# Ordering the experts on the chip, two of them with 64 slots and two products

## The chip, the cores and the metric

One NeuronCore of a Trainium2 chip. The metric is the device time of one execution, in microseconds (us). The kernel before takes 1795.38 us, the median of 3 runs (1792.59 to 1796.04). For times this close, a difference below 0.2% counts as no difference.

## The reference

Three transformer blocks run one after the other over 256 tokens of width 1024, in float32. The change touches one layer, the mixture of experts in the second block. A router gives each token its two best of 8 experts; each expert is a gated network with three weight matrices:

```python
D_FF, N_EXPERTS, TOP_K = 2816, 8, 2
logits = xt @ router_w                       # 256 tokens x 8 experts
top_val, top_idx = lax.top_k(logits, TOP_K)
gates = softmax(top_val)
# for each expert e, the tokens xb that chose it:
y = (silu(xb @ w1[e]) * (xb @ w3[e])) @ w2[e]
out[token] += gate * y
```

There are 512 pairs of a token and an expert. With these inputs the reference's router gives experts 0 to 7 the counts 27, 81, 40, 116, 33, 68, 72 and 75. All weights of all experts are read: 3 x 1024 x 2816 x 4 bytes x 8, 276.8 MB.

## The kernel before

**Three products for a float32.** TensorE multiplies in a reduced form of float32 here (shown as fp32r). So each operand is split in two parts, hi (the value rounded to that form) and lo (what is left), and `mm3` makes three products: hi x hi, lo x hi, hi x lo. Every weight tile must be split on the way: a DMA brings a raw tile of 128x1024 (a *unit*, half a megabyte), ACT casts it to hi (L715), DVE subtracts to get lo (L716), and PE then makes the products (L741 to L743).

**One expert.** Its tokens are gathered into 128 slots by products with a 0/1 matrix (`gather`, tiles bx). The 22 blocks of 128 hidden columns are taken in 6 groups (five of 4 blocks, one of 2). A group has a first product with w1 (4 units, into the PSUM tile ab), one with w3 (4 units), the gate (`silu` on ACT, L1730, and `hidden` on DVE, L1735), a turning of the 128 slots' hidden values by 4 transposes (`turn`, L1686, then a split into the tile hp by L811 on ACT and L812 on DVE), and a second product with w2 (`second`, 4 units, into acc). The second product of a group is recorded after the first products of the next one. The step from one `hidden` to the next is called a *turn* here: 12 units. At an expert's end the result is split (yp), scattered back to the tokens by products (L1695), and added with its gate on DVE (L1696).

**What sets the order.** The experts come as 0, 1, ..., 7. `in_order` chains the instructions of PE, ACT and DVE in the order in which the program records them, so each of these engines works its queue in that order; POOL and the DMA queue are not in the chains. `Units.take` records the split of a unit some four units ahead of its products, since there are 4 buffers for hi and 4 for lo. Raw tiles have about 20 buffers; SP issues their DMAs (L464, L471) as they come free, so the raw tiles are far ahead.

**A second pass** (`tc.If(cnt > P)`) takes an expert's tokens beyond 128; with the counts above it isn't entered.

Of the kernel before, what the change touches and what calls it, by code (L numbers as in the profile page):

```python
# [12 lines left out]
I32 = mybir.dt.int32  # L13
# [105 lines left out]
def t5_bucket(n):  # L119
# [11 lines left out]
    "cm": [("trilT", 128), ("iota128", 128), ("iota8", 8)],  # L131
# [11 lines left out]
def constants():  # L143
# [19 lines left out]
    put("iota128", np.broadcast_to(1 + np.arange(P, dtype=f), (P, P)))  # L163
    put("iota8", np.broadcast_to(np.arange(8, dtype=f), (P, 8)))
# [134 lines left out]
class RouterX:  # L299
# [77 lines left out]
    def route(s, fill):  # L377
# [3 lines left out]
        s.m8, ix, ixf = keep([P, 2, 8]), keep([P, 2, 8], U32), keep([P, 2, 8])  # L381
        o12, s.AmR, s.pos = keep([P, 2, 2, 8]), keep([P, 2, 8], F32R), keep([P, 2, 8])
# [19 lines left out]
        fill(3)  # L402
        ps = k.mm([P, 2, 8])
# [18 lines left out]
    def count(s):

        k, nc = s.k, s.k.nc
        s.ci, cf, pc = s.keep([P, 1], I32), s.keep([P, 1]), k.mm([P, 8])
        for t in range(2):
            nc.tensor.matmul(pc, lhsT=s.ones, rhs=s.AmR[:, t], start=(t == 0), stop=(t == 1))
        nc.vector.tensor_reduce(cf, pc, axis=AX.X, op=ALU.max)
        nc.vector.tensor_copy(s.ci, cf)


class Units:
# [3 lines left out]
    def __init__(s, k):  # L436
        T = k.A["moe"]
        s.k, s.early, s.where, s.n, s.loaded, s.ready = k, {}, {}, 0, 0, []
        s.todo = []
        todo2 = []  # L440
        for e in range(NE):
            u = 0
            for g0 in range(0, FF // P, 4):
                n = min(4, FF // P - g0)
                for i in range(2 * n):
                    s.todo.append((T[e, u + i // 2], i % 2, 8 // n, n * P, i % n * (8 // n)))
                u += n
                s.todo += todo2
                todo2 = [(T[e, u + i // 2], i % 2, 1, D, g0 + i) for i in range(n)]
                u += n // 2  # L450
        s.todo += todo2

    def load(s, n, pool=None):
        src, i, kp, w, _ = s.todo[n]
        k, cs = s.k, slice(i * D, i * D + D)
        s.loaded = max(s.loaded, n + 1)
# [5 lines left out]
        if i == 0 and isinstance(at, Halves) and n + 1 not in s.early and n + 1 not in s.where:  # L462
# [4 lines left out]
            s.early[n + 1] = (raw[:, D:], *s.todo[n + 1][2:4])  # L467
# [70 lines left out]
class K:  # L538
# [163 lines left out]
    def split(s, raw, kper, n, pad=0, to=None):  # L702
# [13 lines left out]
        nc.vector.tensor_tensor(out=lo[:, :m], in0=raw[:, :m], in1=hi[:, :m].bitcast(F32), op=ALU.subtract)  # L716
# [747 lines left out]
    def block2b(s):  # L1464
        with ExitStack() as st:
# [7 lines left out]
            with s.phase("gm", b8=2, b2=2, ring=(ring, 10), ps=dict(mm=InTurn(ps[:4]), acc=InTurn(ps[4:6]), fil=InTurn(ps[6:]))):  # L1473
# [4 lines left out]
                nc.gpsimd.memset(keep([P, 72]), 0.0)  # L1478
# [6 lines left out]
            with s.phase("moe", b1=3, ps=dict(mm=InTurn(ps[:2]), ab=InTurn(ps[2:6]), acc=InTurn(ps[6:])), extra=(("bx", 4),)):  # L1485
                s.raws = raws
                s.sh, s.hp, s.yp = [InTurn([b4[i]]) for i in (0, 1, 3)]

                units.where = {units.loaded + len(raws) + i: p for i, p in enumerate((s.yp, InTurn(b4[2:3])))}
# [607 lines left out]
```

## Time and profile before

| | |
|---|---|
| median of 3 runs | 1795.38 us |
| the profiled execution | 1799.04 us, of which the span of the trace is 1797.2 us |
| stage of the experts' products | about 640 to 1417 us in the span |
| PE, DVE, ACT, POOL busy over the span | 1763.1, 1387.8, 1136.7, 94.5 us |
| bytes moved by DMA | 446.51 MB |

The span is the time from the first instruction to the last; the profiled execution has 1.8 us more around it and stands 3.7 us above the median. Engines are PE (TensorE's products), PEld (its weight loads, beside PE), DVE, ACT and POOL; SP issues the DMAs. A long kernel is read by stages: `windows` give each engine's busy time in a stretch, `waits` say who waited for whom, and timelines list single instructions with their start and length. Lengths of neighbours on one engine overlap a little, since an engine starts on the next instruction before the last one's results are all written; so what one costs in a full queue is the distance of starts, not the length.

### The profile page before, as it was taken

The numbers are of one execution on the slowest core, as the hardware profiler recorded it, in microseconds if no ns is written. First come the engines' busy times: TensorE is split into PE (matmuls) and PEld (weight loads), VectorE is DVE, ScalarE is ACT, GpSimd is POOL, SyncE is SP. The second block draws the span as 40 slices with busy tenths as digits, with TensorE's granted clock in tenths as the row PEclk, the third lists the DMA queues.
The fourth block names the chain that finished last, engine by engine and source line by source line (L and its number), as shares of the span: only waits on it lengthen the run. The fifth ranks groups of instructions, "written<-read, shape, count | busy, mean of one in ns | idle before, by whom it ended". The sixth has DMA issues, their size and how long they took to land. (4 is left out here: it accounts for less than half of the span.)

```text
span 1797.2 us, 26971 instructions
## 1 busy us (share of the span) xinstructions
PE 1763.1 (98%) x10129; PEld 1530.3 (85%) x10129; DVE 1387.8 (77%) x2013; ACT 1136.7 (63%) x1566; POOL 94.5 (5%) x102
## 2 busy tenths in 40 slices
PE   8999999999999999999999999999999899999998
PEld 7889879899987888888888888888888688889997
DVE  6576779755567689999989899999999788865544
ACT  6355656644456478777777787777878665554443
POOL 1100010101000110000000000000000020001101
PEclk9899999999999999999999999999999899999999
DMA  8535463856647679999999999998997444257540
GB/s 288 179 129 165 147 197 118 272 177 192 201 133 258 260 264 362 359 368 337 360 358 369 347 345 371 353 383 319 370 369 285 157 147 153 71 175 250 185 141 24
DMA packets 127947, 446.51 MB, mean 248 GB/s; under 512 B 11304, under 2 KB 23856, under 8 KB 96960
## 3 DMA queue, kind: packets, MB, share of 16 engines
q1 hardware_dynamic: 127808, 444.71, 69.0%
q8 instruction: 81, 1.33, 0.3%
q14 instruction: 58, 0.48, 0.1%
HBM read 443.61 MB, written 2.63 MB: 248 GB/s over the span
## 5 line engine op out<-in xcount | busy, mean ns | idle before, releaser
L716 DVE TENSOR_TENSOR lo<-raw,hi 128x1024 fp32r<-128x1024 f32 (+1 forms) x828 | 987.7, 1223 | 299.5 <-ACT hi L715 289.1
L715 ACT CAST hi<-raw 128x1024 fp32r<-128x1024 f32 (+1 forms) x828 | 852.4, 1048 | 436.7 <-PE mm L743 129.7
L741 PE MATMUL ab<-hi,bx 128*128 128x512 f32 (+1 forms) x768 | 290.7, 378 | 0.0
L743 PE MATMUL ab<-lo,bx 128*128 128x512 f32 (+1 forms) x768 | 286.0, 372 | 0.0
L742 PE MATMUL ab<-hi,bx 128*128 128x512 f32 (+1 forms) x768 | 285.6, 372 | 0.0
L741 PE MATMUL mm<-Xh,hi 128*128 128x256 f32 x760 | 213.9, 281 | 2.2 <-DVE Xl L815 2.2
L743 PE MATMUL mm<-Xl,hi 128*128 128x256 f32 x760 | 213.5, 281 | 0.0
L742 PE MATMUL mm<-Xh,lo 128*128 128x256 f32 x760 | 213.4, 281 | 0.0
L743 PEld LDWEIGHTS ab<-lo,bx 128*128 128x128 f32 x768 | 144.6, 188 | 25.8
L742 PEld LDWEIGHTS ab<-hi,bx 128*128 128x128 f32 x768 | 145.0, 189 | 23.7
L741 PEld LDWEIGHTS ab<-hi,bx 128*128 128x128 f32 x768 | 144.9, 189 | 23.7
L743 PEld LDWEIGHTS mm<-Xl,hi 128*128 128x128 f32 x760 | 145.7, 192 | 0.1
L741 PEld LDWEIGHTS mm<-Xh,hi 128*128 128x128 f32 x760 | 142.9, 188 | 3.3 <-ACT hi L715 2.5
L742 PEld LDWEIGHTS mm<-Xh,lo 128*128 128x128 f32 x760 | 143.1, 188 | 0.9
L741 PE MATMUL acc<-hi,hp 128*128 128x512 f32 x352 | 137.3, 390 | 0.0
L742 PE MATMUL acc<-hi,hp 128*128 128x512 f32 x352 | 137.1, 390 | 0.0
L743 PE MATMUL acc<-lo,hp 128*128 128x512 f32 x352 | 136.9, 389 | 0.0
L741 PE MATMUL fil<-Xh,hi 128*128 128x256 f32 (+1 forms) x352 | 101.8, 289 | 1.3 <-ACT b L1986 0.5
L743 PE MATMUL fil<-Xl,hi 128*128 128x256 f32 (+1 forms) x352 | 100.3, 285 | 0.0
L742 PE MATMUL fil<-Xh,lo 128*128 128x256 f32 (+1 forms) x352 | 100.3, 285 | 0.0
L743 PEld LDWEIGHTS acc<-lo,hp 128*128 128x128 f32 x352 | 66.1, 188 | 13.9
L741 PEld LDWEIGHTS acc<-hi,hp 128*128 128x128 f32 x352 | 66.1, 188 | 13.1
(496 smaller groups left out, 2796.2 us busy)
## 6 DMA issues: line engine op xcount, KB each, us to landing
raw<-in_moe_dram SPq DMA_DIRECT2D x240, 1024.0 KB, 7.1
raw<-in_ffn_w_dram SPq DMA_DIRECT2D x66, 512.0 KB, 4.5
raw<-in_moe_dram SPq DMA_DIRECT2D x48, 512.0 KB, 6.6
raw<-in_a_w_in_dram SPq DMA_DIRECT2D x24, 512.0 KB, 4.4
raw<-in_w_gate_dram SPq DMA_DIRECT2D x22, 512.0 KB, 4.4
raw<-in_w_up_dram SPq DMA_DIRECT2D x22, 512.0 KB, 4.8
raw<-in_w_down_dram SPq DMA_DIRECT2D x22, 512.0 KB, 3.7
raw<-in_w_in_odd_dram SPq DMA_DIRECT2D x20, 512.0 KB, 4.7
```

The source lines that it names most:

```text
L715: nc.scalar.copy(hi[:, :m], raw[:, :m])
L716: nc.vector.tensor_tensor(out=lo[:, :m], in0=raw[:, :m], in1=hi[:, :m].bitcast(F32), op=ALU.subtract)
L741: nc.tensor.matmul(out, lhsT=lh, rhs=rh, start=start, stop=False, skip_group_check=skip)
L742: nc.tensor.matmul(out, lhsT=ll, rhs=rh, start=False, stop=False, skip_group_check=skip)
L743: nc.tensor.matmul(out, lhsT=lh, rhs=rl, start=False, stop=stop, skip_group_check=skip)
```

## The change

Four things change in the stage of the experts.

- **Order on the chip.** Experts 0 and 1 keep their places. The other six are ordered by the number of their tokens, fewest first (`order`), and the gates, positions and counts are made again for the new places. SP loads the six numbers into registers, and weight addresses follow from them.
- **Narrow experts.** Those at places 2 and 3 (here experts 4 and 2, with 33 and 40 tokens) get 64 slots. The hi parts of their 64 slots and the lo parts stand side by side in one operand of 128 columns, so `prods` makes two products (with hi and with lo of the weights) where `mm3` makes three. The two halves are added when the hidden values are turned: 8 products with a folding matrix take the place of 4 transposes, and the gate comes after it, on 64 slots.
- **Pairs in turn.** The places are taken in the pairs (0, 1), (2, 4), (5, 6), (3, 7), and the two of a pair take turns group by group, so a narrow group and a wide one alternate in the second and the fourth pair. ab has 2 PSUM banks instead of 4, acc 4 instead of 2.
- **Every eighth subtraction on POOL.** `fetch` gives the subtraction for lo of units 7, 15, 23, ... to POOL instead of DVE: 66 of 528.

The second pass is entered where a wide expert has more than 128 tokens or a narrow one more than 64.

```diff
@@ Units.fetch, split @@
-            hi, lo = s.k.split(*(s.early.pop(s.n, None) or s.load(s.n, s.where.get(s.n))))
+            k = s.k
+            hi, lo = k.split(*(s.early.pop(s.n, None) or s.load(s.n, s.where.get(s.n))),
+                             sub=k.nc.gpsimd if s.n % 8 == 7 else k.nc.vector)
...
-        nc.vector.tensor_tensor(out=lo[:, :m], in0=raw[:, :m], in1=hi[:, :m].bitcast(F32), op=ALU.subtract)
+        (sub or nc.vector).tensor_tensor(out=lo[:, :m], in0=raw[:, :m], in1=hi[:, :m].bitcast(F32), op=ALU.subtract)
@@ the order of pairs and groups @@
+PAIRS = ((0, 1), (2, 4), (5, 6), (3, 7))
+NARROW = (2, 3)
+GROUPS = [(g, min(4, FF // P - g)) for g in range(0, FF // P, 4)]
+TURNS = [(pair, i, g, n) for pair in PAIRS
+         for i, (g, n) in [(i, g) for g in GROUPS[:-2] for i in range(2)] + [(i, g) for i in range(2) for g in GROUPS[-2:]]]
@@ RouterX @@
+    def order(s):
+        k, nc = s.k, s.k.nc
+        s.ci, s.ix = s.keep([P, 1], I32), s.keep([P, 8], U32)
+        key, top, by = k.ts(8), k.ts(8), k.ts(8)
+        nc.vector.tensor_tensor(out=key, in0=k.c("rank"), in1=s.counts(), op=ALU.subtract)
+        nc.vector.max(top, key)
+        nc.vector.max_index(s.ix, top, key)
+        nc.vector.tensor_copy(by, s.ix)
+        nc.vector.tensor_tensor(out=s.o12, in0=by[:, None, None, :].to_broadcast([P, 2, 2, 8]),
+                                in1=s.ixf[:, :, 0:2, None].to_broadcast([P, 2, 2, 8]), op=ALU.is_equal)
+        nc.vector.tensor_tensor(out=s.AmR, in0=s.o1, in1=s.o2, op=ALU.add)
+        s.shares()
...
+    def experts(s):
+        s.of = [0, 1] + [s.k.nc.values_load(s.ix[0:1, c:c + 1].bitcast(I32), engines=[mybir.EngineType.SP], min_val=0, max_val=NE - 1)
+                         for c in range(2, NE)]
@@ block2b: banks of PSUM @@
-            with s.phase("moe", b1=3, ps=dict(mm=InTurn(ps[:2]), ab=InTurn(ps[2:6]), acc=InTurn(ps[6:])), extra=(("bx", 4),)):
+            with s.phase("moe", b1=3, ps=dict(mm=InTurn(ps[:2]), ab=InTurn(ps[2:4]), acc=InTurn(ps[4:])), extra=(("bx", 4),)):
@@ experts @@
+        def prods(g, out, x, hi, lo, start, stop):
+            if len(x) == 1:
+                nc.tensor.matmul(out, lhsT=x[0], rhs=hi, start=start, stop=False)
+                nc.tensor.matmul(out, lhsT=x[0], rhs=lo, start=False, stop=stop)
+            else:
+                s.mm3(out, *x, hi, lo, start, stop)
...
         def turn(g, last=False):
+            if g.narrow:
+                ps, n = s.mm([P, 2, 4, 64]), g.n
+                for q in range(2):
+                    for c in range(n):
+                        nc.tensor.matmul(ps[:, q, c], lhsT=g.sh[:, q, c * P:(c + 1) * P], rhs=s.c("fold"),
+                                         start=(q == 0 and c == 0), stop=True, skip_group_check=True)
+                hp = s.hp.tile([P, 4, 2, 64], F32R, tag="hp", name=s.nm("hp"))
+                g.hp = [hp.rearrange("p c q n -> p c (q n)")]
+                sl, hd = (g.sh[:, q, :n * 64].rearrange("p (c n) -> p c n", n=64) for q in range(2))
+                nc.scalar.activation(sl, ps[:, 0, :n], AF.Silu)
+                nc.vector.tensor_tensor(out=hd, in0=ps[:, 1, :n], in1=sl, op=ALU.mult)
+                nc.scalar.copy(hp[:, :n, 0], hd)
+                nc.vector.tensor_tensor(out=hp[:, :n, 1], in0=hd, in1=hp[:, :n, 0].bitcast(F32), op=ALU.subtract)
+                return
...
-            nc.scalar.activation(g.sh[:, 0, :n], g.a[:, :n], AF.Silu, scale=g.r)
+            nc.scalar.activation(g.sh[:, 0, :n], g.a[:, :n], AF.Copy if g.narrow else AF.Silu, scale=g.r)
...
-            nc.vector.scalar_tensor_tensor(g.hd[:, :n], g.b[:, :n], g.r, g.sh[:, 0, :n], op0=ALU.mult, op1=ALU.mult)
+            if g.narrow:
+                nc.scalar.activation(g.hd[:, :n], g.b[:, :n], AF.Copy, scale=g.r)
+            else:
+                nc.vector.scalar_tensor_tensor(g.hd[:, :n], g.b[:, :n], g.r, g.sh[:, 0, :n], op0=ALU.mult, op1=ALU.mult)
```

What this makes of the engines' queues is shown at three places. The first is DVE's queue. In the kernel before, between two `hidden` (L1735), all 12 subtractions of a turn are there, with the turned values' lo (L812) after the fifth:

```order
L1735 SCALAR_TENSOR_TENSOR sh_8578<-ab_8580,sm_8415,sh_8578 128x512
L716 TENSOR_TENSOR lo_8640<-raw_8620,hi_8639 128x1024
L716 TENSOR_TENSOR lo_8652<-raw_8649,hi_8651 128x1024
L716 TENSOR_TENSOR lo_8664<-raw_8661,hi_8663 128x1024
L716 TENSOR_TENSOR lo_8676<-raw_8673,hi_8675 128x1024
L716 TENSOR_TENSOR lo_8687<-raw_8673,hi_8686 128x1024
L812 TENSOR_TENSOR hp_8701<-mm_8696,hp_8701 128x512
L716 TENSOR_TENSOR lo_8707<-raw_8704,hi_8706 128x1024
```

After the change, in a turn that follows a narrow group (L761 is the subtraction, L1764 and L1766 are the gate and the lo of the folded values, L1822 is `hidden` of the wide group), DVE has:

```order
L761 TENSOR_TENSOR lo_8893<-raw_8890,hi_8892 128x1024
L1764 TENSOR_TENSOR sh_8816<-mm_8913,sh_8816 128x256
L1766 TENSOR_TENSOR hp_8922<-sh_8816,hp_8922 128x4x64
L761 TENSOR_TENSOR lo_8930<-raw_8927,hi_8929 128x1024
...
L761 TENSOR_TENSOR lo_8999<-raw_8996,hi_8998 128x1024
L1822 SCALAR_TENSOR_TENSOR sh_8961<-ab_8963,sm_8635,sh_8961 128x512
L761 TENSOR_TENSOR lo_9020<-raw_9017,hi_9019 128x1024
```

The subtraction for hi_8903, between the first two of these rows, and the one for hi_9009, beside the last `hidden`, have left DVE.

The second place is POOL's queue, which before has nothing in this stage. Now it holds them, one behind the other with nothing between:

```order
L761 TENSOR_TENSOR lo_8596<-raw_8576,hi_8595 128x1024
L761 TENSOR_TENSOR lo_8734<-raw_8714,hi_8733 128x1024
L761 TENSOR_TENSOR lo_8820<-raw_8806,hi_8819 128x1024
L761 TENSOR_TENSOR lo_8904<-raw_8890,hi_8903 128x1024
```

Since POOL is in no chain, each of them can start as soon as its hi is cast.

The third place is PE's queue at the end of a narrow group's first products (two a step, L1738 and L1739) and the second product of the wide group before it (three, L786 to L788):

```order
L1738 MATMUL ab_8818<-hi_8819,bx_8273 128x512
L1739 MATMUL ab_8818<-lo_8820,bx_8273 128x512
L1738 MATMUL ab_8818<-hi_8819,bx_8273 128x512
L1739 MATMUL ab_8818<-lo_8820,bx_8273 128x512
L786 MATMUL acc_8856<-hi_8829,hp_8785 128x512
L787 MATMUL acc_8856<-hi_8829,hp_8785 128x512
L788 MATMUL acc_8856<-lo_8830,hp_8785 128x512
```

A unit of a narrow group thus gives PE 4 products instead of 6; the number of units, and so of DMAs, casts and subtractions, is what it was.

## Rows read from the trace of the kernel before

**Rows 1.** Windows: a stretch of the stage; each engine's busy us, clock, DMA, GB/s.

```profile
core 0: us, PE busy (x) PEld busy (x) DVE busy (x) ACT busy (x) POOL busy (x), PEclk, DMA share, GB/s
1150.00:1200.00 50.00, 50.00 (x228) 41.38 (x227) 46.34 (x44) 39.71 (x42) 0.00 (x0) 1.00 0.98 374
```

**Rows 2.** Waits in 640 to 1400 us: us in total, times, longest.

```profile
ACT hi L715 <- PE acc L742: 53.4, 150, 1.0
DVE lo L716 <- ACT hi L715: 41.2, 76, 1.4
ACT hi L715 <- DMA raw<-in_moe_dram: 0.6, 2, 0.3
```

**Rows 3.** Waits of the DMA queue in 540 to 1400 us.

```profile
SPq L464 <- DVE lo L716: 584.2, 226, 10.3
```

**Rows 4.** Windows: one pair of experts, from `hidden` to `hidden`; then L716 alone.

```profile
846.60:1040.50 193.90, 193.90 (x942) 163.10 (x941) 179.38 (x177) 151.42 (x166) 0.00 (x0) 1.00 0.95 358
...
846.60:1040.50 193.90, 155.47 (x133) 1.00 0.95 358
```

**Rows 5.** Timeline of PE: start, us, engine, line, operation.

```profile
1394.48 0.39 PE L741 MATMUL acc<-hi,hp 128*128 128x512 f32 x1
...
1395.84 0.39 PE L741 MATMUL acc<-hi,hp 128*128 128x512 f32 x1
```

**Rows 6.** Timeline of DVE in one turn; in brackets, idle before.

```profile
895.81 0.74 DVE L1735 SCALAR_TENSOR_TENSOR sh<-ab,sm,sh 128x512 f32<-128x512 f32 x1
896.48 6.09 DVE L716 TENSOR_TENSOR lo<-raw,hi 128x1024 fp32r<-128x1024 f32 x5
902.91 0.69 DVE L812 TENSOR_TENSOR hp<-mm,hp 128x512 fp32r<-128x512 f32 x1 [0.34 <-ACT hp L811]
903.86 3.50 DVE L716 TENSOR_TENSOR lo<-raw,hi 128x1024 fp32r<-128x1024 f32 x3 [0.26 <-ACT hi L715]
912.60 0.75 DVE L1735 SCALAR_TENSOR_TENSOR sh<-ab,sm,sh 128x512 f32<-128x512 f32 x1
```

**Rows 7.** Groups of DVE by line and shape, 640 to 1400 us: count, busy, mean ns.

```profile
L1735 DVE SCALAR_TENSOR_TENSOR sh<-ab,sm,sh 128x512 f32<-128x512 f32 x40 | 29.9, 746 | 0.0
L812 DVE TENSOR_TENSOR hp<-mm,hp 128x512 fp32r<-128x512 f32 x39 | 26.9, 690 | 8.3 <-ACT hp L811 8.2
L812 DVE TENSOR_TENSOR hp<-mm,hp 128x256 fp32r<-128x256 f32 x7 | 2.9, 418 | 0.0
```

**Rows 8.** Timelines of POOL and of DVE where both work, at 49 us.

```profile
49.03 5.67 POOL L985 TENSOR_TENSOR b<-b,b 128x2048 f32<-128x2048 f32 x1 [5.26 <-DMA b<-relskew]
...
48.98 1.23 DVE L716 TENSOR_TENSOR lo<-raw,hi 128x1024 fp32r<-128x1024 f32 x1 [1.08 <-ACT hi L715]
51.70 5.22 DVE L716 TENSOR_TENSOR lo<-raw,hi 128x1024 fp32r<-128x1024 f32 x2 [1.49 <-ACT hi L715]
```

**Rows 9.** The same timelines at 376 and 559 us.

```profile
376.60 1.81 POOL L819 TENSOR_TENSOR b<-b,b 128x512 fp32r<-128x512 f32 x1 [17.69 <-ACT b L818]
...
376.03 1.23 DVE L716 TENSOR_TENSOR lo<-raw,hi 128x1024 fp32r<-128x1024 f32 x1 [0.41 <-ACT hi L715]
377.17 0.68 DVE L1278 TENSOR_TENSOR b<-mm,b 128x512 f32<-128x512 f32 x1
...
559.25 3.32 POOL L1530 TENSOR_TENSOR wst<-wst,cm 128x1024 f32<-128x1024 f32 x1 [4.39 <-DMA cm<-in_cm_dram]
...
559.09 1.23 DVE L716 TENSOR_TENSOR lo<-raw,hi 128x1024 fp32r<-128x1024 f32 x1
```

**Rows 10.** Rate of the DMA engines, 600 to 650 us in 40 slices.

```profile
GB/s 419 459 419 406 410 111 23 0 0 105 256 419 59 0 105 419 315 0 66 347 413 13 0 157 426 298 246 302 419 419 419 256 7 85 334 419 397 23 0 0
```

**Rows 11.** Windows around the start of the stage: busy us, clock.

```profile
632.00:639.10 7.10, 5.43 (x30) 4.11 (x30) 6.71 (x32) 3.29 (x7) 2.51 (x2) 1.00 0.95 345
639.10:642.50 3.40, 3.40 (x16) 3.40 (x17) 2.22 (x5) 1.16 (x3) 0.00 (x0) 0.50 0.35 87
```

**Rows 12.** SP's loads of a register before the second pass.

```profile
L1610 SPq TENSOR_LOAD <-keep x1: 479/479/479, 1413.0 to 1413.0; - x1
```

More of the change, by code (lines that the diff above doesn't have):

```diff
@@ new lines, in gates, with shares, counts @@
+        s.shares()
+    def shares(s):
+        nc = s.k.nc
+        for t in range(2):
+            nc.vector.tensor_scalar(s.gt[:, t], s.o1[:, t], s.g12[:, 0, t:t + 1], None, op0=ALU.mult)
+            nc.vector.scalar_tensor_tensor(s.gt[:, t], s.o2[:, t], s.g12[:, 1, t:t + 1], s.gt[:, t], op0=ALU.mult, op1=ALU.add)
+    def counts(s):
+        pc = s.k.mm([P, 8])
+        for t in range(2):
+            s.k.nc.tensor.matmul(pc, lhsT=s.ones, rhs=s.AmR[:, t], start=(t == 0), stop=(t == 1))
+        return pc
@@ L422, in count @@
     def count(s):
         k, nc = s.k, s.k.nc
[L425 to L429, printed above, removed]
+        cf, top = k.ts(8), k.ts(1)
+        nc.vector.tensor_scalar(cf, s.counts(), -128.0, None, op0=ALU.add)
+        nc.vector.tensor_scalar(cf[:, 2:4], cf[:, 2:4], 64.0, None, op0=ALU.add)
@@ L1596, in gm @@
         pp = pq.tile([P, 2, D], F32, tag="pp", name=s.nm("pp"))
-        rest = [lambda nb=nb, t=t: s.halve(pp, nb, sums[nb], (t,)) for nb in range(2) for t in range(2)] + [x.count]
+        rest = [lambda nb=nb, t=t: s.halve(pp, nb, sums[nb], (t,)) for nb in range(2) for t in range(2)] + [x.order, x.slots, x.count, x.experts]
         units.ahead(3)
@@ L1653, in slots @@
             return r, GT[:, i]
-        return [onehots] + [lambda j=j: chunks(j) for j in range(0, 8, 2)], [[OfTwo(X[q], i) for q in range(2)] for i in range(2)], slots
+        return [onehots] + [lambda j=j: chunks(j) for j in range(0, 8, 2)], ops, slots
     def experts(s, units, rest=None):
@@ L1677, in first @@
                 for k, hi, lo in units.take():
-                    s.mm3(out[:, :n], X[0][k], X[1][k], hi, lo, k == 0, k == 7)
+                    prods(g, out[:, :n], [x[k] if isinstance(x, OfTwo) else x[:, k] for x in X], hi, lo, k == 0, k == 7)
                 if u in hooks:
@@ new lines, in work @@
+                g = Group()
+                g.c, g.g0, g.n, g.y = pair[i], g0, n, y[i]
+                g.narrow = g.c in narrow
+                end = g0 + n == nblocks and i == 1
+                give = lambda i=i: got[i].extend(slots(i))
+                hooks = {}
+                if prev is not None:
+                    hooks[0] = lambda g=prev: turn(g)
+                if at == 0:
+                    hooks = {0: todo[3], 1: lambda: (todo[4](), late[2]()), 2: lambda: (late[3](), give())}
+                elif at == 1:
+                    hooks = {0: late[0], 1: lambda: (late[1](), give()), 2: hooks[0]}
+                elif g0 == 0:
+                    hooks[1] = give
@@ new lines, in work @@
+                if end and pair != PAIRS[-1]:
+                    nxt = s.gather(PAIRS[PAIRS.index(pair) + 1], narrow)
+                    hooks[1] = nxt[0][0]
+                g.a = s.ps("ab")
+                first(g, X[i], g.a, hooks)
+                g.r, g.GT = got[i]
+                if at:
+                    silu(g)
+                g.b = s.ps("ab")
+                first(g, X[i], g.b, {} if at else {1: lambda g=g: silu(g)})
+                hidden(g)
+                hooks = {}
+                if end and pair == PAIRS[-1]:
+                    hooks[1] = lambda g=g: turn(g, True)
+                elif end:
+                    hooks = dict(enumerate(nxt[0][1:]))
@@ L1792, in work @@
+                if 2 <= at <= 5:
+                    hooks[1] = late[2 + at]
+                if prev is not None:
+                    second(prev, hooks)
+                prev = g
             second(prev, {})
```

147 lines of the change are left out of this document (67 added, 80 removed).

## The prediction

> **What bounds the kernel now.** I read the windows over the stage of the experts first, then who waits for whom, then one pair of experts, then single timelines. In the windows PE is busy for the whole of a stretch of 50 us at the full clock, while DVE has 46.3 us and the DMA engines 0.98 of theirs: PE is the bound, and DVE is 7% behind it [rows 1]. The waits say the same from the other side. ACT's cast waits for PE to give back a buffer of hi (53.4 us for acc alone), DVE's subtraction waits for the cast (41.2 us), and the cast hardly ever waits for a DMA (0.6 us) [rows 2]. SP's queue stands still until a subtraction frees a raw tile, 584 us in all: the DMAs are paced by the consumers [rows 3]. So a gain on PE is a gain in time only down to the next bound, and the question is where DVE stands then.
>
> One pair of experts takes 193.9 us: PE 193.9, DVE 179.4 of which 155.5 are its subtractions, ACT 151.4 [rows 4]. I take it for each of the four pairs and work by the pair.
>
> **PE's part.** Six products take 1.36 us, 0.227 each [rows 5]; I take half of that for the products of half the width in an expert's last group. A narrow expert loses one product in three: 16 groups of 8 for w1 and w3 less the small ones, that is 80 of full and 16 of half width, and 44 for w2. That is 124 x 0.227 + 16 x 0.113 = 30.0 us. The folding products (8 of 64 columns for 4 of 128) have as many columns as the transposes; no row here shows them, so they cost between nothing and 8 weight loads' worth more, 0 to 1 us a group, of which PE has 30 us to give. PE alone would need 163.9 us for each of the two pairs with a narrow expert, and the change would be worth 60 us.
>
> **DVE's part, and POOL's.** DVE's queue packs subtractions at 1.14 us: three in 3.50, of which the last has its whole 1.22 [rows 6]. The 132 subtractions of a pair are then 150.5 us, with the other 23.9 us (179.4 less 155.5, [rows 4]) 174.4. Were nothing moved to POOL, that would be the next bound, 10.5 us above PE's 163.9. The change takes an eighth of the subtractions, 16.5 a pair, off DVE: 18.8 us less. But POOL and DVE do not work side by side on such tiles here. At 49 us POOL has a product of 2048 columns. DVE's subtraction in front of it ends at 50.21, and POOL, which started at 49.03, ends at 54.70, 4.49 after that. The two subtractions that DVE starts at 51.70 take 5.22 instead of the 2.36 that two take, and end 2.22 after POOL does: DVE has stood still until POOL was done [rows 6, 8]. At 376 us POOL waits the other way round, for the subtraction that ends at 377.26, and ends 1.15 later (512 columns); and at 559 us its product of 1024 columns ends 2.25 after DVE's subtraction at 560.32 [rows 9]. So a subtraction of 128x1024 on POOL holds DVE's subtractions off for 2.25 us. A subtraction that DVE makes takes 1.14. An operation of DVE that reads PSUM is not held off: L1278 runs its 0.68 us beside POOL at 377 us [rows 9].
>
> The Trainium skill (SBUF — State Buffer, section "SBUF: two separate sides") says that the pair of ports which VectorE and GpSimd share is an exclusive lock held for a whole instruction, against a VectorE operation with two SBUF inputs too. The rows above agree, to 0.1 us. By that rule the move costs the time worked out here; if the two shared the port's bandwidth or did not meet at all, the move would be worth the 18.8 us a pair.
>
> Now the sum for a pair with a narrow expert. DVE: 115.5 subtractions at 1.14, 131.7 us. Its other work: 23.9 less 3.6, since six narrow turns have a gate and an lo of 256 columns (0.42 each) for `hidden` and an lo of 512 (0.75 and 0.69) [rows 7]; 20.3 us. POOL: 16.5 x 2.25 = 37.1 us in which no subtraction of DVE runs. Together 189.1 us if nothing of DVE's other work falls beside POOL, 168.8 if all of it does. I take 189.1, the upper end, for this reason: POOL isn't in the chain, so it asks as soon as the cast of its unit is done. When DVE lags, ACT's cast of a unit is done about two subtractions before DVE gets there, POOL gets in at the next boundary, and DVE's next instruction there is another subtraction; the queue has only L1764 or `hidden` near two of three such places, and a little later than that. So PE's 30 us shrink to 193.9 - 189.1 = 4.8 us a pair, 9.6 for both.
>
> A pair of two wide experts: 131.7 + 23.9 + 37.1 = 192.7 us for DVE and POOL, against PE's 193.9. It stays PE's, with no slack to speak of: before, DVE idled 0.3 to 0.7 us at several places of a turn [rows 6], and a subtraction that is held off for a microsecond comes after its product is due when scatter or gather stands in the queue as well. Bounds: nothing, and 16.5 x 1.11 = 18.3 us a pair if every delay reached PE; I take 0.5 us a pair, near the lower end, as the four buffers of lo cover about three units of 1.36 us. That is 1 us.
>
> `order`, `slots`, `count` and `shares` are new in the first pair: some 25 instructions of DVE on 8 or 16 columns. In three places DVE's queue waits for a small product that stands behind a unit in PE's queue, and the subtractions stand behind it. Bounds 0 and 3 x 1.36 + 25 x 0.2, 9 us; I take 2. The six register loads on SP cost 0.48 us each, 2.9 in all [rows 12], and lie in SP's waits; only the next DMA stands behind them, and raw tiles are many units ahead. ACT gets a cast of b and a gate of 256 columns a narrow group, under 1.5 us a group or 9 a pair on top of 151.4, still under 189. Nothing else of the program changes.
>
> Sum: -9.6 + 1 + 2 = -6.6 us. The profiled execution of before, 1799.0 us, would become 1792.4; as it stands 3.7 us above the median of the runs, I predict 1795.4 - 6.6 = 1788.8, say 1789 us.
>
> **The rivals.**
> *POOL's work does lie beside DVE's.* If DVE's PSUM work and its idle places fall in POOL's windows for the most part, say 14 of the 20.3 us, a narrow pair takes 175 us: 2 x 14 us more, about 1761 us. For it: `hidden` and L1764 do stand next to POOL's units. Against: POOL asks earlier than they come. 0.17.
> *The wide pairs pay.* The place is an expert's end, where DVE has scatter, yp and gather on top; the price is two POOL units with 1.11 us more each at 8 ends, 17.8 us; and it decides as soon as DVE's delay there is over the microsecond or so that the buffers of lo cover. Net -6.6 + 17.8, about 1807 us. For it: 192.7 against 193.9. Against: the pair of before has two such ends and PE without a gap [rows 4]. 0.17.
> *The clock.* In the 7.1 us before 639.1 PE had 1.7 us of gaps, and then the granted clock was 0.50, or 1.2 GHz, for 3.4 us [rows 11]. In a narrow pair PE would stop for 2 us wherever POOL holds DVE off. One such stretch in each of 11 narrow turns loses 1.7 us each, 19 us: about 1808. Against: PE was busy for 0.76 of those 7.1 us, and would be for 163.9 of 189.1, 0.87, of a narrow pair. 0.08.
> *The DMA is the bound anyway.* A pair has 69.2 MB; at the 358 GB/s of now [rows 4] that is 193 us, and nothing is gained: 1796 us. Against: 374 GB/s over 50 us [rows 1], and 419 where the queue was free to run [rows 10]; and 189 us need only 366. 0.10. The Trainium skill (SBUF — State Buffer, section "SBUF: two separate sides") gives about 358 GB/s for HBM to one core, by which no pair could be faster than it is; the trace does not agree, with its 374 [rows 1].
> *A second pass.* With the counts of the reference 116 is the most of a wide expert and 40 of a narrow one, so the change does what it says; a second pass would add over 700 us. Under 0.01.
>
> **How the numbers follow.** My case has 0.48 and a range of its own from 1780 to 1798. A difference under 0.2%, 3.6 us, is no difference that the measurement tells. Of the 0.48, 0.33 lie below 1791.8, 0.10 within, 0.05 above 1799. Faster: 0.33 + 0.17 + 0.02 of the DMA's case, 0.52. Same: 0.10 + 0.07 of the DMA's + 0.02 of the wide pairs', 0.19. Slower: 0.05 + 0.15 + 0.08 + 0.01, 0.29. The range to 8 in 10 takes in most of the overlap case and of the two slower ones: 1762 to 1811 us.
>
> **What would show it.** Right: in the second and fourth pair PE's windows have 0.85 to 0.9 of busy time and DVE's are full; subtractions next to a POOL unit take about 3.4 us in the timeline; POOL's take 2.4 to 3.5; a narrow pair lasts 186 to 192 us, a wide one 194 to 196. Wrong: DVE's subtractions at 1.22 beside POOL's and a narrow pair under 180 us; or waits of the cast for DMAs of tens of us; or a clock of 0.50 inside the stage.

## The result, and the profile after

The changed kernel takes 1816.8 us (median of 4 runs, 1813.92 to 1819.71) against 1795.7 us for the kernel before in the same comparison: ratio 1.0114 [1.0082, 1.0145], about 1.1% slower. I had predicted 1789, a little faster, with a range from 1762 to 1811. The span of its profiled execution is 1813.4 us, 16.2 more than before.

To see where, I cut the stage of the experts at the first small reduction of each pair (L1651 before, L1712 after, the first `slots`) and at the start of the last scatter's addition on DVE. From that first point to that last one ("the stage") it is 767.9 us before and 784.0 after: 16.1 us, all of the difference of the spans. These are the windows pair by pair, of the kernel before and then of the changed one (columns as in [rows 1]; the second and fourth pair of the changed kernel have a narrow expert; the last line of the second ends 0.7 us early):

```profile
650.40:838.10 187.70, 187.70 (x915) 157.91 (x915) 172.42 (x171) 148.15 (x163) 0.00 (x0) 1.00 0.93 348
838.10:1032.00 193.90, 193.90 (x942) 163.10 (x941) 179.37 (x178) 151.42 (x166) 0.00 (x0) 1.00 0.95 358
1032.00:1225.90 193.90, 193.90 (x942) 163.10 (x941) 179.37 (x178) 151.41 (x166) 0.00 (x0) 1.00 0.95 358
1225.90:1418.30 192.40, 191.12 (x909) 159.23 (x907) 175.81 (x174) 147.51 (x161) 0.00 (x0) 1.00 0.83 317
```

```profile
649.40:845.20 195.80, 190.56 (x917) 157.28 (x916) 172.67 (x175) 148.32 (x167) 41.75 (x16) 1.00 0.89 334
845.20:1040.00 194.80, 182.12 (x869) 142.59 (x868) 172.27 (x162) 151.81 (x178) 46.86 (x17) 1.00 0.93 356
1040.00:1239.70 199.70, 195.62 (x940) 162.17 (x939) 177.44 (x167) 151.51 (x170) 42.60 (x16) 1.00 0.92 347
1239.70:1432.70 193.00, 179.67 (x836) 139.88 (x835) 168.54 (x155) 147.96 (x173) 47.33 (x17) 0.99 0.83 316
```

The two wide pairs are longer by 8.1 and 5.8 us, and PE, which had no gap before, has 4 to 5 us of them. The pairs with a narrow expert, which were to fall to 189.1 us, take 194.8 and 193.7 where [rows 4] have 193.9. PE idles in them, as it should. But DVE is busy for only 172.3 of 194.8 us: it isn't full, and that speaks against my sum at once. Of the signs that I had named, POOL's times (2.36 to 3.49 us) and the subtractions beside it (up to 3.3 us) came; a full DVE and a narrow pair of 186 to 192 us did not.

POOL's hold on DVE is as [rows 8, 9] foretold. DVE in the second pair, then POOL there, then PE's wait (start, length, and in brackets the idle time before and what ended it):

```profile
874.83 5.50 DVE L761 TENSOR_TENSOR lo<-raw,hi 128x1024 fp32r<-128x1024 f32 x4
880.25 0.68 DVE L857 TENSOR_TENSOR hp<-mm,hp 128x512 fp32r<-128x512 f32 x1
880.86 13.61 DVE L761 TENSOR_TENSOR lo<-raw,hi 128x1024 fp32r<-128x1024 f32 x10
896.59 0.42 DVE L1764 TENSOR_TENSOR sh<-mm,sh 128x256 f32<-128x256 f32 x1 [2.13 <-ACT sh L1763]
897.49 0.42 DVE L1766 TENSOR_TENSOR hp<-sh,hp 128x256 fp32r<-128x256 f32 x1 [0.47 <-ACT hp L1765]
```

```profile
883.44 3.13 POOL L761 TENSOR_TENSOR lo<-raw,hi 128x1024 fp32r<-128x1024 f32 x1 [7.59 <-ACT hi L760]
```

```profile
886.62 0.50 PE L1739 MATMUL ab<-lo,bx 128*128 128x512 f32 x1 [1.02 <-POOL lo L761]
```

Ten subtractions take 13.61 us instead of 11.4: one of them stands beside POOL's and waits 2.2 us for it. By the Trainium skill (SBUF — State Buffer, section "SBUF: two separate sides") the pair of ports is held for a whole instruction; the row agrees to 0.1 us. Then something comes that I had not counted: DVE stands for 2.13 us before L1764, the gate of the folded values. It waits for ACT's L1763, and that for PE's folding products (L1758). The waits of the stage show it as a chain (total, times, longest), with PE's and its weight loads' waits for POOL and the gather's below:

```profile
ACT sh L1763 <- PE mm L1758: 22.8, 12, 2.3
DVE sh L1764 <- ACT sh L1763: 20.9, 12, 2.2
PEld ab L1739 <- POOL lo L761: 16.3, 10, 2.2
PE ab L1739 <- POOL lo L761: 12.2, 10, 1.9
PE acc L1739 <- POOL lo L761: 4.7, 8, 1.0
ACT bx L856 <- DVE bx L857: 10.1, 8, 2.0
```

PE's products of narrow groups (L1739) thus stand for 16.9 us behind a lo from POOL. The last line is in the gather for a pair with a narrow expert, where PE stands still for 1.93 us. ACT's second cast of a product waits for DVE's subtraction from the first part of it, though both only read the same PSUM tile; DVE makes that subtraction behind one for a unit. In PE's timeline this gap, and one of the waits for POOL:

```profile
836.52 0.70 PE L1779 MATMUL mm<-yp,b 128*128 128x512 f32 x2 [1.93 <-DVE bx L857]
849.21 0.50 PE L1739 MATMUL ab<-lo,bx 128*128 128x512 f32 x1 [1.94 <-POOL lo L761]
```

The granted clock is 0.50 (1.2 GHz) in the stage for only 3.4 us, at 1244.2.

### The profile page after: what moved, and what is told of

Same layout as the page of the kernel before. It is cut to its first block, busy times and chain, and to the rows that moved or that the text cites. A ratio compares the mean times of both kernels' runs of the same rounds, so it can differ in the third digit from the quotient of the medians.

```text
span 1813.4 us, 27240 instructions
## 1 busy us (share of the span) xinstructions
PE 1744.8 (96%) x9986; PEld 1487.7 (82%) x9986; DVE 1373.6 (76%) x1978; ACT 1137.6 (63%) x1598; POOL 271.6 (15%) x168
## 5 line engine op out<-in xcount | busy, mean ns | idle before, releaser
L761 DVE TENSOR_TENSOR lo<-raw,hi 128x1024 fp32r<-128x1024 f32 (+1 forms) x762 | 967.3, 1302 | 303.5 <-ACT hi L760 298.9
L761 POOL TENSOR_TENSOR lo<-raw,hi 128x1024 fp32r<-128x1024 f32 x66 | 178.5, 2705 | 614.2 <-ACT hi L760 476.4
L786 PE MATMUL ab<-hi,bx 128*128 128x512 f32 (+1 forms) x576 | 218.1, 379 | 0.0
L788 PE MATMUL ab<-lo,bx 128*128 128x512 f32 (+1 forms) x576 | 215.6, 374 | 1.5 <-POOL lo L761 1.3
L786 PE MATMUL mm<-Xh,hi 128*128 128x256 f32 x760 | 214.3, 282 | 1.9 <-DVE Xl L860 1.9
L787 PE MATMUL ab<-hi,bx 128*128 128x512 f32 (+1 forms) x576 | 214.3, 372 | 0.2 <-DVE bx L857 0.2
L788 PE MATMUL mm<-Xl,hi 128*128 128x256 f32 x760 | 213.8, 281 | 0.0
L786 PEld LDWEIGHTS mm<-Xh,hi 128*128 128x128 f32 x760 | 143.2, 188 | 3.2 <-ACT hi L760 2.3
L788 PEld LDWEIGHTS mm<-Xl,hi 128*128 128x128 f32 x760 | 145.6, 192 | 0.0
L788 PEld LDWEIGHTS ab<-lo,bx 128*128 128x128 f32 x576 | 108.4, 188 | 24.6 <-POOL lo L761 3.1
L787 PEld LDWEIGHTS ab<-hi,bx 128*128 128x128 f32 x576 | 108.6, 189 | 18.8 <-DVE bx L857 0.5
L786 PEld LDWEIGHTS ab<-hi,bx 128*128 128x128 f32 x576 | 108.6, 188 | 17.0
L788 PE MATMUL acc<-lo,hp 128*128 128x512 f32 x264 | 103.5, 392 | 0.5 <-DVE lo L761 0.2
L786 PE MATMUL acc<-hi,hp 128*128 128x512 f32 x264 | 103.4, 392 | 0.0
L787 PE MATMUL acc<-hi,hp 128*128 128x512 f32 x264 | 103.1, 390 | 0.0
L786 PE MATMUL fil<-Xh,hi 128*128 128x256 f32 (+1 forms) x352 | 101.6, 289 | 1.3 <-ACT b L2075 0.5
L788 PE MATMUL fil<-Xl,hi 128*128 128x256 f32 (+1 forms) x352 | 100.1, 284 | 0.0
L1739 PE MATMUL ab<-lo,bx 128*128 128x512 f32 (+1 forms) x192 | 77.3, 409 | 16.4 <-POOL lo L761 12.2
```

The lines of the kernel that those rows point to most:

```text
L761: (sub or nc.vector).tensor_tensor(out=lo[:, :m], in0=raw[:, :m], in1=hi[:, :m].bitcast(F32), op=ALU.subtract)
L786: nc.tensor.matmul(out, lhsT=lh, rhs=rh, start=start, stop=False, skip_group_check=skip)
L787: nc.tensor.matmul(out, lhsT=ll, rhs=rh, start=False, stop=False, skip_group_check=skip)
L788: nc.tensor.matmul(out, lhsT=lh, rhs=rl, start=False, stop=stop, skip_group_check=skip)
L1739: nc.tensor.matmul(out, lhsT=x[0], rhs=lo, start=False, stop=stop)
```

## The experiments

Eighteen kernels in five comparisons, each beside the kernel before (1796.5 to 1799.4 us there). Stage as defined above, from one profile of each. I take it as the better measure of one change, since the time ahead of the stage takes about 645 us in some profiles and about 651 in others, with nearly the same code there.

| kernel | median us | ratio to before | stage us |
|---|---|---|---|
| before | 1795.7 | | 767.9 |
| the change | 1816.8 | 1.0114 [1.0082, 1.0145] | 784.0 |
| a_no_pool | 1793.3 | 0.9981 [0.9968, 0.9995] | 762.5 |
| a_casts_first | 1811.4 | 1.0081 [1.0056, 1.0106] | 777.5 |
| a_no_narrow | 1810.6 | 1.0073 [1.0046, 1.0100] | 779.9 |
| a_pairs_only | 1802.7 | 1.0035 [1.0019, 1.0051] | 772.2 |
| c_static | 1799.7 | 1.0021 [1.0004, 1.0037] | 771.6 |
| c_before_pool | 1807.8 | 1.0066 [1.0041, 1.0091] | 778.1 |
| b_pool_wide | 1798.6 | 1.0009 [0.9992, 1.0025] | 769.5 |
| d_pool_wide_units | 1802.0 | 1.0018 [1.0001, 1.0035] | 770.3 |
| b_np_casts | 1787.7 | 0.9937 [0.9918, 0.9956] | 756.8 |
| b_between | 1793.6 | 0.9988 [0.9971, 1.0005] | 766.0 |
| c_spread | 1784.3 | 0.9929 [0.9905, 0.9954] | 752.4 |
| c_spread_between | 1798.5 | 1.0011 [0.9996, 1.0025] | 766.3 |
| d_five_plain | 1773.2 | 0.9872 [0.9842, 0.9901] | 745.8 |
| d_five | 1772.9 | 0.9861 [0.9830, 0.9891] | 743.7 |
| d_five_between | 1795.9 | 0.9994 [0.9978, 1.0009] | 767.9 |
| e_before_five | 1797.1 | 0.9992 [0.9975, 1.0009] | 767.7 |
| e_after_five | 1831.5 | 1.0187 [1.0158, 1.0216] | 797.3 |

**The parts of the change.** One edit each, or two:

```diff
# a_no_pool
-                             sub=k.nc.gpsimd if s.n % 8 == 7 else k.nc.vector)
+                             sub=k.nc.vector)
# a_no_narrow; a_pairs_only has both edits
-NARROW = (2, 3)
+NARROW = ()
# a_casts_first: gather, for a pair with a narrow expert
...
+            for hi, lo, pp in parts:
+                nc.scalar.copy(hi, pp)
+            for hi, lo, pp in parts:
+                nc.vector.tensor_tensor(out=lo, in0=pp, in1=hi.bitcast(F32), op=ALU.subtract)
```

a_no_pool: 

> The changed kernel with all subtractions for lo on DVE. Theory A (a subtraction on POOL holds DVE's off for 2.25 us, and that bounds the narrow pairs): two turns of a narrow pair go from 33.2 us to about 31, the 1.9 us gap of PE behind the POOL unit after 846.8 us goes, and the wide pairs lose their stalls; 1788 us, 1782 to 1795. Theory B (the narrow group's own chain of casts, gate and lo across three engines is the cost, and POOL's units lie beside other work): no gain, 1813 to 1822 us, or slower, since DVE takes back 66 subtractions of 1.14 us.

a_casts_first: 

> The changed kernel, where the gather of a pair with a narrow expert makes both casts of a PSUM tile on ACT before both subtractions on DVE, so that ACT's second cast no longer waits for DVE. If the alternation costs what the trace shows (ACT's casts of bx wait 10.1 us for DVE in 8 waits, and PE stops 1.9 us at 834 us and at 1229 us): 5 us less, 1812 us, 1808 to 1815. If these waits are hidden by other work: 1817 us, within 2.

a_no_narrow: 

> The changed kernel with no narrow expert: order on the chip, pairs in turn and POOL's units stay, all experts have 128 slots and three products. Theory A: PE is the bound again in all pairs, with a few stalls behind POOL's units at the experts' ends: 1802 us, 1797 to 1808. Theory B: 1796 to 1799 us, as before, since the narrow groups' chain is gone.

a_pairs_only: 

> The changed kernel with no narrow expert and no subtraction on POOL: order on the chip and pairs in turn alone. Both theories: 1798 us, 1795 to 1801, the 2 or 3 us over before being the order. What lies between this and the kernel with no narrow expert but with POOL is POOL's cost where PE is the bound: 3 to 9 us by theory A, 0 to 2 by theory B.

Without POOL the loss is gone: 23.5 us of the medians, 21.5 of the stage. The casts came out as expected (5.4 us). With all experts wide POOL still costs 7.9 us of the medians, within theory A's 3 to 9. But a_no_narrow and a_pairs_only both came out above their ranges (1810.6 for up to 1808, 1802.7 for up to 1801): what is left of the change without narrow experts and without POOL costs more than either theory had. The narrow experts save 9.7 us of the stage without POOL (772.2 to 762.5) and cost 4.1 with it (779.9 to 784.0): the two parts of the change work against each other.

**Order on the chip, and POOL alone.**

```diff
# c_static, on a_pairs_only (b_static: the same with the limit of 64 slots left in count)
-        s.of = [0, 1] + [s.k.nc.values_load(s.ix[0:1, c:c + 1].bitcast(I32), ...
+        s.of = list(range(NE))
...
-... + [x.order, x.slots, x.count, x.experts]
+... + [lambda: None, lambda: None, x.count, x.experts]
# c_before_pool, on the kernel before
+                                sub=s.k.nc.gpsimd if s.n % 8 == 7 else s.k.nc.vector)
```

b_static: 

> All experts wide, no POOL, and the experts in their own order: no order on the chip, no register loads, fixed addresses; the pairs in turn by groups and the PSUM banks as changed. With order on the chip it was 1802.7 us. If the pairs in turn cost the 6 us over the kernel before: 1802 us (1800 to 1804). If the order on the chip costs them: 1797 us (1795 to 1798).

c_static: 

> All experts wide, no POOL, experts in their own order by fixed addresses, with no second pass this time; pairs in turn by groups and the PSUM banks as changed. If the pairs in turn cost the 6 us over the kernel before: 1802 us (1800 to 1804), as with the order on the chip. If the order on the chip costs them: 1797 us (1795 to 1798). If the products come 233 ns apart in the stage of the experts, as in the first trace with fixed addresses (227 in the kernel before), 20 us more than either: about 1820 us.

c_before_pool: 

> The kernel before with nothing changed but every eighth subtraction on POOL (66). If POOL's price with wide experts is that of the held-off subtractions, it is the 7.9 us measured with the pairs in turn: 1805 us (1801 to 1808). If it was paid only because the pairs in turn leave DVE less slack: 1797 us (1795 to 1799). If each delay of 1.11 us reached PE: 1870 us.

b_static gave no answer. Expert 3, at place 3 and with 116 tokens, was over that place's limit of 64, so the second pass ran (2612 us). c_static has a stage of 771.6 us, 0.6 less than with the order on the chip, and its median lies between the two expectations. So by the stage the pairs in turn cost 3.7 us and the order 0.6, which is too little to be told from nothing with one profile of each; by the medians alone I could not have told. On the old order POOL costs 9.9 us (10.2 of the stage), near the expectation: its price needs no pairs in turn.

**Where POOL's price is paid.**

```diff
# b_pool_wide: POOL only in the pairs without a narrow expert
+                             sub=k.nc.gpsimd if s.n % 8 == 7 and s.n // 132 in (0, 2) else k.nc.vector)
# d_pool_wide_units: POOL for every eighth unit that is a wide expert's
+                             sub=k.nc.gpsimd if s.n % 8 == 7 and s.todo[s.n][0] not in NARROW else k.nc.vector)
```

b_pool_wide: 

> The full change, but POOL has its subtractions only in the first and third pair, those without a narrow expert (33 of 66). Theory A, POOL's price is paid where DVE is the bound: 1793.3 + half of the 7.9 us that POOL cost with all experts wide, 1797 us (1795 to 1800). Rival, each subtraction on POOL costs the same 0.36 us everywhere (23.5 us for 66): 1805 us (1802 to 1808).

d_pool_wide_units: 

> The full change, but POOL keeps every eighth subtraction only where the unit belongs to a wide expert: about 50 of 66, the 33 of the wide pairs and some 17 in the wide runs of the narrow pairs. With the 33 alone it was 1798.6 us, with all 66 it is 1816.8. Theory A, the price is paid in the narrow runs, where DVE sets the pace: 1800 us (1798 to 1803). Rival, all of POOL's units in a narrow pair cost alike: 1798.6 + 17/33 of 18.2 = 1808 us (1805 to 1811).

Both as theory A has it. By the stage: the 32 units of wide pairs cost 7.0 us (762.5 to 769.5), the 14 of the wide experts in the other pairs 0.8, and the 20 of the narrow experts 13.7, 0.7 us each. The second pair with those 14 on POOL, and with none, has nearly the same length:

```profile
847.10:1035.00 187.90, 181.54 (x869) 142.47 (x869) 168.52 (x172) 151.26 (x178) 18.57 (x7) 1.00 0.94 369
```

```profile
836.70:1024.30 187.60, 181.26 (x869) 142.40 (x868) 174.00 (x179) 151.18 (x178) 0.00 (x0) 1.00 0.95 370
```

**Why a narrow pair isn't shorter without POOL.** In two turns PE takes 12 narrow units in a row (4 products of 0.227, 0.91 us) and then 12 wide ones (1.36 us); DVE needs 1.14 for either. So DVE paces the one run and PE the other, unless buffers carry DVE's lead across. In the run of wide units PE has the 8 folding products of the narrow group too, which show as 16 records. From the first one's start to the next product's they take 1.70 us, where the 4 transposes take 0.35. In the change, then before:

```profile
894.25 1.89 PE L1758 MATMUL mm<-cm,sh 128*128 128x64 f32 x16
895.95 0.48 PE L786 MATMUL ab<-hi,bx 128*128 128x512 f32 x1
```

```profile
884.84 0.60 PE L1686 MATMUL mm<-ck,sh 128*128 128x128 f32 x4
885.19 0.48 PE L741 MATMUL ab<-hi,bx 128*128 128x512 f32 x1
```

An estimate by runs is 12 x 1.14 + 12 x 1.36 + 1.70 = 31.7 us for the two turns, without DVE's other work; from `hidden` to `hidden` they take 31.6 in a_no_pool and b_np_casts. Experiments on the order of the queue and on the buffers follow:

```diff
# b_np_casts: a_no_pool and a_casts_first together; the base of all below
# b_between: the second product of the group before between w1's and w3's
+            s.todo += ab[:n] + todo2 + ab[n:] if between(pair, i, g0, n) else ab + todo2
...
+                if alt:
+                    second(prev, {1: late[2 + at]} if 2 <= at <= 5 else {})
                 g.b = s.ps("ab")
...
# c_spread: the turning in steps (c_spread_between: both)
...
-                    hooks[0] = lambda g=prev: turn(g)
...
+                    hooks[0] = lambda g=prev: steps.extend(turn(g))
...
+                        hooks[1] = lambda: (steps[0](), then())
+                        hooks[2] = lambda: steps[1]()
...
# d_five_plain: a fifth buffer of hi and lo (d_five on c_spread, d_five_between on b_between)
-                raws = s.raws[at:] + s.raws[:at] + [sp] * 4 + [xw, xt]
+                raws = s.raws[at:] + s.raws[:at] + [sp] * 4
...
+                s.his, s.los = s.his + [xw], s.los + [xt]
```

b_np_casts: 

> The change without POOL, and in the gather of a pair with a narrow expert both casts of a product ahead of both subtractions. If the wait in the gather is of its own (1.52 us of PE at 826.4 in the run without POOL, at two gathers): 3 us less than without POOL, 1790 us (1787 to 1792). If the gather was late only because of POOL: 1793 us, as without POOL.

b_between: 

> The same, and the second product of the group before stands between a group's first product with w1 and the one with w3, so that narrow and wide units take turns by 4 and no longer by 12. Theory A: in a run of 12 narrow units DVE is the bound (12 subtractions of 1.14 us), in a run of 12 wide ones PE (12 of 1.36), and four buffers of hi and lo cannot carry work from one run to the other; two turns of 31.6 us become about 30.3, 8 times, 10 us less: 1779 us (1775 to 1784). Rival B: DVE's sum over two turns is the bound in any order: 1788 to 1791 us. Rival C: the second product comes too close behind the turning of its hidden values and PE waits for hp: 1792 us or more.

c_spread: 

> No POOL, casts first in the gather, and the turning of hidden values recorded in steps: the products after unit 0 as now, the gate (or the split of a wide group) after unit 1, hi and lo of a narrow group after unit 2. Theory A: DVE's 2.1 us of idle time at the folding chain in every two turns of a narrow pair (31.6 us) come from where the chain stands in its queue; the two turns become about 30.2, 8 times, some 10 us less than 1787.7: 1778 us (1774 to 1783). Rival B: in the run of 12 wide units PE is the bound and DVE would wait for a buffer instead of the chain: 1787 us (1785 to 1790).

c_spread_between: 

> The same with the second product between the first products with w1 and w3 (narrow and wide units in turn by 4). If its 1.27 us of PE's idle time in every two turns came from the turning of the hidden values, which stood at once before the waiting product: 5 us less than with the second product last, 1775 us (1770 to 1780). If DVE's sum (29.5 us in 31.4) is the bound whatever the order: 1786 to 1793 us, as it was (1793.6) or a little less.

d_five_plain: 

> No POOL, casts first in the gather (1787.7 us), and five buffers of hi and of lo instead of four (two raw tiles are given up for them). Theory A, DVE's lead from the wide run is lost at four buffers: two turns of 31.6 us become about 30.5, 8 times, 9 us less: 1779 us (1775 to 1783). Rival B, waits inside DVE's queue: 1787 us (1785 to 1790). Rival C, two raw tiles less make the cast wait for DMAs: 1792 us or more.

d_five: 

> Five buffers, and the turning of hidden values recorded in steps (1784.3 us with four). Theory A: 9 us less, 1775 us (1771 to 1780). Rival B: 1784 us (1781 to 1787).

d_five_between: 

> Five buffers and narrow and wide units in turn by 4 (1793.6 us with four buffers, turning recorded at once). If a fifth buffer carries the lead over runs of 4: 1780 us (1775 to 1785). If hidden only stands behind one more subtraction and PE waits for it longer: 1794 to 1800 us.

The gather's wait was of its own: 5.7 us of the stage. The other orders of the queue failed, and not all in the way that a rival had. b_between and c_spread_between got no shorter turns (31.4 us); a new wait came instead, PE's transposes behind `hidden`, and that behind the subtractions that DVE records ahead of it. In b_between PE, then DVE:

```profile
876.47 0.66 PE L1777 MATMUL mm<-ck,sh 128*128 128x128 f32 x4 [1.27 <-DVE sh L1829]
```

```profile
872.27 3.49 DVE L763 TENSOR_TENSOR lo<-raw,hi 128x1024 fp32r<-128x1024 f32 x3
875.67 0.74 DVE L1829 SCALAR_TENSOR_TENSOR sh<-ab,sm,sh 128x512 f32<-128x512 f32 x1
```

The 9.2 us of the stage that b_between loses to b_np_casts lie elsewhere, though: its narrow pairs are as long (187.5 and 186.0 us for 187.7 and 185.6), its two wide pairs 4.4 and 4.6 longer. The third pair of b_np_casts, then of b_between:

```profile
1027.00:1221.70 194.70, 194.25 (x941) 162.66 (x940) 179.11 (x183) 151.46 (x170) 0.00 (x0) 1.00 0.94 356
```

```profile
1031.60:1230.90 199.30, 196.05 (x941) 162.29 (x940) 180.98 (x183) 151.44 (x170) 0.00 (x0) 1.00 0.93 349
```

c_spread_between (1798.5 us, above both of its expectations) and d_five_between (1795.9, as its second one has it) have wide pairs as long as these. So these kernels say little about whether runs of 4 are better for a narrow pair.

c_spread moved DVE's idle time from L1764 to the next subtraction (1.37 us, for a cast that waits for its buffer); the turns stayed at 31.6 us, as its rival said, and its 3.4 us of the median can't be told from b_np_casts by the intervals. (The stage is 4.4 us shorter, most of it in the narrow pairs, ahead of their first full turns.) The fifth buffer did it: 11.0 us of the stage and 14.5 of the medians less than b_np_casts, more than the 9 expected, and 1.3% faster than the kernel before. d_five, with the turning in steps as well, is the same within the intervals. DVE in two turns without POOL, with four buffers (a_no_pool) and with five (d_five_plain):

```profile
871.62 13.71 DVE L761 TENSOR_TENSOR lo<-raw,hi 128x1024 fp32r<-128x1024 f32 x12
886.29 0.42 DVE L1764 TENSOR_TENSOR sh<-mm,sh 128x256 f32<-128x256 f32 x1 [0.95 <-ACT sh L1763]
887.18 0.42 DVE L1766 TENSOR_TENSOR hp<-sh,hp 128x256 fp32r<-128x256 f32 x1 [0.47 <-ACT hp L1765]
888.14 8.21 DVE L761 TENSOR_TENSOR lo<-raw,hi 128x1024 fp32r<-128x1024 f32 x7 [0.53 <-ACT hi L760]
```

```profile
860.20 0.74 DVE L1829 SCALAR_TENSOR_TENSOR sh<-ab,sm,sh 128x512 f32<-128x512 f32 x1
860.85 5.76 DVE L762 TENSOR_TENSOR lo<-raw,hi 128x1024 fp32r<-128x1024 f32 x5
866.53 0.69 DVE L858 TENSOR_TENSOR hp<-mm,hp 128x512 fp32r<-128x512 f32 x1
867.13 13.71 DVE L762 TENSOR_TENSOR lo<-raw,hi 128x1024 fp32r<-128x1024 f32 x12
880.75 0.42 DVE L1771 TENSOR_TENSOR sh<-mm,sh 128x256 f32<-128x256 f32 x1
881.64 0.43 DVE L1773 TENSOR_TENSOR hp<-sh,hp 128x256 fp32r<-128x256 f32 x1 [0.47 <-ACT hp L1772]
882.60 8.12 DVE L762 TENSOR_TENSOR lo<-raw,hi 128x1024 fp32r<-128x1024 f32 x7 [0.53 <-ACT hi L761]
890.63 0.74 DVE L1829 SCALAR_TENSOR_TENSOR sh<-ab,sm,sh 128x512 f32<-128x512 f32 x1
```

From `hidden` to `hidden`, 860.20 to 890.63, it is 30.4 us with 24 subtractions of 1.14: DVE idles for 1.0 us and is the bound at last. Against four buffers the two turns lose 1.14 us, one subtraction. PE is not far off: its own 12 x 0.91 + 12 x 1.36 + 1.70 + 0.35 are 29.3. The second pair in b_np_casts, then in d_five_plain:

```profile
839.30:1027.00 187.70, 181.38 (x869) 142.42 (x868) 174.06 (x179) 151.24 (x178) 0.00 (x0) 1.00 0.94 370
833.20:1015.70 182.50, 178.35 (x869) 143.67 (x868) 173.48 (x179) 149.73 (x178) 0.00 (x0) 1.00 0.96 380
```

**Controls with the fifth buffer.** The same edit on the kernel before and on the full change:

e_before_five: 

> The kernel before with five buffers of hi and lo instead of four. Theory A, the buffer carries DVE's lead from a run of wide units to one of narrow ones, and the kernel before has no narrow ones: no difference, 1798 us (1795 to 1800). Rival: the buffer helps any order of the experts: 1784 us (1780 to 1790).

e_after_five: 

> The full change, POOL and gather as they are (1816.8 us), with five buffers. Two turns of a narrow pair are 33.2 us with four buffers; 21 subtractions of DVE at 1.14, 3 of POOL at 2.25 and 2.2 us of DVE's other work are 32.9. If this sum is the bound, the buffer gives almost nothing there: 1812 us (1808 to 1816). If POOL's price is a want of lead: 1816.8 - 14.5 = 1802 us (1799 to 1806).

The kernel before gains nothing from it, as the theory wants. The full change gets 14.7 us slower, which neither expectation had. POOL, DVE and PE there at 876 us, and the clock in two windows, the first from inside PE's gap on:

```profile
875.92 9.10 POOL L762 TENSOR_TENSOR lo<-raw,hi 128x1024 fp32r<-128x1024 f32 x1 [9.25 <-ACT hi L761]
```

```profile
875.92 6.89 DVE L762 TENSOR_TENSOR lo<-raw,hi 128x1024 fp32r<-128x1024 f32 x6
888.40 2.57 DVE L762 TENSOR_TENSOR lo<-raw,hi 128x1024 fp32r<-128x1024 f32 x2 [5.59 <-ACT hi L761]
```

```profile
879.12 0.39 PE L1740 MATMUL ab<-hi,bx 128*128 128x512 f32 x1
885.07 0.80 PE L1741 MATMUL ab<-lo,bx 128*128 128x512 f32 x1 [5.55 <-POOL lo L762]
885.66 0.63 PE L1740 MATMUL ab<-hi,bx 128*128 128x512 f32 x1
```

```profile
881.40:888.20 6.80, 3.13 (x7) 2.49 (x8) 1.41 (x2) 1.45 (x2) 3.61 (x1) 0.50 0.30 102
918.90:922.30 3.40, 3.40 (x10) 2.65 (x9) 3.40 (x4) 1.87 (x3) 0.00 (x0) 0.51 0.90 340
```

Here POOL asked as DVE began six subtractions in a row, and got in only when DVE's queue ran dry: it ends at 885.02, 2.2 us after them. PE waited 5.55 us for that one lo, and the clock stood at 0.50 for 6.8 us, from 881.4 on, still within that gap. In the next turns PE's gaps are 2.1 us, each with 3.4 us at half clock behind it. In the whole stage the clock is at 0.50 for 30.7 us, against 3.4 in the change. Half of the 27.3 us between them, 13.7, is the most that this can have added, and the stage is 13.3 longer; how much of it is the clock and how much the waits themselves no run separates. So POOL's price is no fixed sum: as I read these rows, it is who gets the port, PE's wait for the unit that comes late, and the clock behind that wait.

## Why the prediction was wrong

The difference in the stage, 16.1 us, comes apart by single edits, made in this order: pairs in turn +3.7, order on the chip +0.6, narrow experts -9.7, POOL +21.5. I had -6.6 in all.

- **"Together 189.1 us" for a narrow pair.** This is the step that failed most: -9.6 us forecast for both, +2.2 measured (194.8 and 193.7 against 193.9 and 192.4). The hold of 2.25 us was right. Wrong was to take the larger of two sums over a pair, and to take the upper end of DVE's. DVE is busy for 172.3 us with the held-off time in it. Less the 131.7 and 20.3 of its own work that leaves 20.3, so of POOL's 37.1 us hardly more than half fell on DVE's subtractions; the rest lay beside its idle time and other work, where I had put none. Even so the pair takes 194.8, since neither sum sets its length: DVE's and POOL's work has to be done where the narrow units are, 12 in a row, and DVE stands idle for 22.5 us of the pair, 10.4 of it before L1764, where it waits for PE's folding products. Shown by the place: POOL's 20 units of narrow experts cost 13.7 us, the 14 of their partners 0.8; and by the fifth buffer, which takes 5.2 us off each such pair (187.7 in b_np_casts to 182.5) and nothing off the kernel before. It is not the whole account: without POOL my sum for DVE would have been 150.5 + 20.3 = 170.8, and the 11.7 us that are left with five buffers I did not trace.
- **"0 to 1 us a group" for the folding products.** 1.35 us more than the transposes, 1.70 for 0.35, so about 7.4 us a pair by 5.5 groups. PE's own 163.9 us become 171.3, as much as my sum for DVE without POOL, and the 1.70 us stand in the run that PE paces. "As many columns" was no measure of them.
- **"I take 0.5 us a pair" for POOL in the wide pairs.** 3.5 measured, 7.0 for both. The rival of the wide pairs had the sign, at 17.8 us; the kernel before with POOL alone pays 10.2 for its four pairs. Whether the place is the experts' ends, as the rival had it, isn't shown: in that kernel's trace PE's visible waits for POOL's lo come to 3.2 us in the stage.
- **"Nothing else of the program changes."** The gather of a narrow pair does: its two parts are cast and subtracted in turn from one PSUM tile, and that cost 5.7 us of the stage (a_no_pool to b_np_casts; 6.5 in the full change). It lies in the wide pairs, before each narrow one; the third pair falls from 197.5 to 194.7. The lines are in the change, though not among those shown of it above, and no term stood for them.
- **"I take 2" for the order on the chip.** 0.6. That the pairs take turns by groups, with other banks of PSUM, had no term and cost 3.7; which of the two it is stays open.
- **The rivals.** The DMA was not the bound: 380 GB/s over a narrow pair in d_five_plain. The clock fell once, for 3.4 us; its mechanism came only in e_after_five. That POOL's work would lie beside DVE's came true for about half of it (above), but not that the pair gets shorter by it.

The change holds two parts of opposite worth, and the forecast doesn't say so, though its own numbers do: 170.8 us for a narrow pair without POOL, 189.1 with it. Without POOL's part and with the casts in order it is 0.6% faster than the kernel before, and with a fifth buffer 1.3%.

## What to carry to other kernels

Where two kinds of work alternate in long runs and each has another engine as its bound, add the runs, not the engines' sums: only as much is hidden as the buffers between carry over, and one buffer more can be worth as much as the products saved (11.0 and 9.7 us of the stage here). Before work is moved to an engine that shares a port, price it where the other engine sets the pace, and look at the waits of the third engine for the result that comes late. A change of several parts is forecast part by part, with a term for every changed line that issues an instruction.

## What the runs showed of the hardware

When both ask for the port, POOL sometimes gets in behind the subtraction that runs (883.44 in the change: done in 3.13 us) and sometimes only behind six (9.10 us at 875.92 in e_after_five). In the change none of POOL's 66 takes more than 3.49 us; in e_after_five four take 4.06 to 9.10. What decides it no run shows.

In b_static the products of the stage came 233 ns apart (the 227 of [rows 5] in all others), at a granted clock of 1.00; in c_static, which differs in the limit of slots and one small tile, they were 227 again. Its first pass took 786.5 us for 771.6. The cause is open.
